# Four small edits to the order of a macaron encoder layer: one estimate for attention keys, a sum before splits, and the last two output units

## The chip, the cores and the metric

The kernel runs as one program on one core of a Trainium2 chip. The metric is the device time of one execution in microseconds (us). Engines are named as in the profile: PE is TensorE (PEld its weight loads), DVE is VectorE, ACT is ScalarE, POOL is GpSimd and SP is SyncE, which here only issues DMAs.

## The reference

One layer on 512 tokens of width 1024, all float32:

```python
h = modulate(rmsnorm(x, norm_ffn1), sh1, sc1)
x = x + 0.5 * g1 * swiglu(h, w_ffn1_in, w_ffn1_out)          # first block
h = modulate(rmsnorm(x, norm_mix), sh2, sc2)
qa, ka, va, qb, kb, vb, ga, gb = split(h @ w_in)
ya = window_gqa_sink(rope(rmsnorm(qa)), rope(rmsnorm(ka)), va, sink) @ w_branch_a
ob = diff_attention(rope(rmsnorm(qb)), rope(rmsnorm(kb)), vb, lam)
yb = (rmsnorm(ob) * (1 - lam_init)) @ w_branch_b
x = x + g2 * ((sigmoid(ga) * ya + sigmoid(gb) * yb) @ w_out)
h = modulate(rmsnorm(x, norm_ffn2), sh3, sc3)
x = x + 0.5 * g3 * swiglu(h, w_ffn2_in, w_ffn2_out)          # second block
```

The shifts, scales and gates `sh1` to `g3` come from `silu(c) @ w_mod + b_mod`; the inner width of both SwiGLU blocks is 2816.

## The kernel before

**Splits.** Each float32 operand of a matmul is split into a high part (ACT casts it) and a low part (DVE subtracts the cast from the source), and each product takes three matmuls: high by high, high by low, low by high. A weight chunk is loaded by SP into one of five `raw` buffers or into a `u4` buffer, cast (L481) and subtracted (L482) into one of five places of the pair `high`, `low`. A `u4` or `raw` chunk may then be changed in place by an accumulating DMA that POOL issues (L488), which makes the next weight sum out of it.

**Second block in units of seven products.** A `Unit` computes a 512 by 512 block of a product by Winograd's scheme: seven products (`s1`, `a11`, `a12`, `s2`, `s4`, `s3`, `a22`) in place of eight. `BANK` gives each product a PSUM bank: `a11`, `s2`, `s3` and `a22` of a unit are added up one after the other in bank `x`, `s1` and `s4` in `v`, `a12` in `w`. Between them bank `x` is read: ACT copies it after `a11` and `s2` (L510), and after `s3` DVE adds it to an earlier copy (L516), so that `a22` of the same unit can start only behind that sum. `after` holds these reads, `post` what becomes of a finished quarter. For the outgoing units `post` is in `out_unit` (L1706, one update of the residual stream per 128 rows, then a DMA to the output once a row block is complete).

**What sets the order there.** `items` is a list of products in the order in which PE does them. `run_items` walks it. `ASK` and `MAKE` say how many products ahead of its use a weight is loaded and split; `begin(starts[n])` issues what is due, and holds a split back while all five high/low places are taken. Only POOL's order is the program's; the order of PE, DVE, ACT and SP in the second block is made when the program is built, by a scheduler with estimates of its own. `copies` ties each weight cast behind the latest copy of a bank.

The list ends with the two outgoing units `end[0]` and `end[1]` (the last three row pairs of the hidden width, output rows 0 to 511 and 512 to 1023): both `s1` and both `a11` for the rows that are ready, the rest of these for the last row pair, then `a12`, `s2`, `s4`, `s3`, `a22`, each for both units in turn.

**Attention.** PE's, DVE's and ACT's order between the two blocks is written by `Line`, a list of pieces with due times in estimated us. Projections run as the main work, and a piece whose due time has come is put between two groups of their matmuls. `keys` normalises and rotates the keys of one block of 128 tokens and puts the turn of that block (a transpose on PE into the one bank `tp`, L1199, read by an ACT cast and a DVE subtract, L169 and L170) at `line.helped(...) + SLACK`, whose first number is the DVE time that is assumed. It serves the 8 key heads of the differential attention (`keys_b`, which runs first) and the 2 key heads of the window attention (`keys_a`, the second attention, under the projection `w_qa`).

Of the kernel before, what the change touches and what calls it, by code (L numbers as in the profile page):

```python
# [15 lines left out]
ALU = mybir.AluOpType  # L16
# [16 lines left out]
SH1, SC1, G1, SH2, SC2, G2, SH3, SC3, G3 = range(9)  # L33
# [64 lines left out]
RAW, HILO, F2 = 5, 5, 8  # L98
# [11 lines left out]
PERIOD_A, PERIOD_B, SLACK = 6.5, 3.6, 0.8  # L110
# [10 lines left out]
H = T // 2  # L121
# [3 lines left out]
def layer(ctx: ExitStack, tc: tile.TileContext, a: dict):  # L125
    nc = tc.nc
    V, S, G, PE = nc.vector, nc.scalar, nc.gpsimd, nc.tensor
# [14 lines left out]
    def f2():  # L142
        return sbuf("f2", [P, T], F32, F2)
# [10 lines left out]
    def bank(tag):  # L154
        return psum.tile([P, T], F32, name=name(tag), tag=tag, bufs={"acc": 3, "op": 1, "sc": 3, "tp": 1}[tag])
# [17 lines left out]
    turn, holders = [0], {}  # L173
# [11 lines left out]
    def let_go(holder):  # L185
        for i in [i for i in holders if holders[i] == holder]:
            del holders[i]
# [30 lines left out]
    begin = keep([P, 6 * NC], "begin")  # L218
    crow = u4(F32).rearrange("p a b -> p (a b)")[0:1, :]
    nc.scalar.dma_start(crow, a["c"].unsqueeze(0))  # L220
    x = [xt() for _ in range(NC)]
# [4 lines left out]
    parts, modv = [], []  # L226
# [198 lines left out]
    MAKE = {"s1": 5, "a11": 3, "a12": 2, "s2": 4, "s4": 2, "s3": 2, "a22": 3}  # L425
    T1, T2 = HALVES

    def two(po, w, k, x, first, last):

        (wh, wl), (xh, xl) = w, x  # L430
        for j in range(2):
            s = slice((2 * k + j) * P, (2 * k + j + 1) * P)
            out = po[:, j * H : (j + 1) * H]
            PE.matmul(out, wh[:, s], xh, start=first and j == 0, stop=False, skip_group_check=True)  # L434
            PE.matmul(out, wh[:, s], xl, start=False, stop=False, skip_group_check=True)  # L435
            PE.matmul(out, wl[:, s], xh, start=False, stop=last and j == 1, skip_group_check=True)  # L436

    copies = []

    class Unit:  # L440
# [8 lines left out]
            self.tags = {"w": "tp" if odd else "op"}  # L449

        asked = ("s1", "a11", "a12", "a22")
        copied = ()
        spare, apart, more = ("s1",), (), {"s1": ("s2", "a11"), "s2": ("s4", "a12"), "a11": ("s3", "a21")}

        def place(self, q):
# [35 lines left out]
        def multiply(self, q, ks=None):  # L491
            b = BANK[q]
            ks = range(self.depth) if ks is None else ks
            if b not in self.bank:
                self.bank[b] = bank(self.tags.get(b) or ("sc" if self.odd else "acc"))
            po = self.bank[b]
            new = not any(BANK[d] == b for d in self.done)
            for k in ks:
                x = self.operand(OPERAND[q], k)
                two(po, self.ready[q], k, x, new and k == 0, k == self.depth - 1)  # L500
            if self.depth - 1 in ks:
                let_go((self, q))

        def after(self, q):

            v, b = self.v, self.bank
            self.done.add(q)
            if q in ("a11", "s1", "s2"):
                v[q] = f2()
                copies.append(S.copy(v[q], b["v" if q == "s1" else "x"]).ins)  # L510
            elif q == "s3":
                t = b["x"]
                if q in self.copied:
                    t = f2()
                    S.copy(t, b["x"])
                V.tensor_tensor(v["s1"], v["s1"], t, ALU.add)  # L516
                self.post("c22", v["s1"], self)
            elif q == "a22":
                self.post("c21", b["x"], self)
            if q in ("a11", "a12") and self.done >= {"a11", "a12"}:  # L520
                V.tensor_tensor(v["a11"], v["a11"], b["w"], ALU.add)
                self.post("c11", v["a11"], self)
            if q in ("s2", "s4") and self.done >= {"s2", "s4"}:
                V.tensor_tensor(v["s2"], v["s2"], b["v"], ALU.add)
                self.post("c12", v["s2"], self)
# [3 lines left out]
    def run_items(items):  # L529

        at, due = 0.0, []
        starts = []
        for n, item in enumerate(items):
            starts.append(at)
            at += item[0]
            if item[1] is None:
                continue  # L540
            u, q = item[1:3]
            for do, ahead in ((u.ask, ASK), (u.prepare, MAKE)):
                if q in ahead:
                    due.append((starts[n] - PRODUCT * ahead[q] - 0.01, len(due), do, q))
        due.sort(key=lambda d: d[0:2])

        def begin(now):

            for d in [d for d in due if d[0] <= now]:
                _, _, do, p = d  # L550
                if do.__name__ == "ask" or p in do.__self__.ready or len(holders) < HILO:
                    due.remove(d)
                    do(p)

        for n, (cost, u, q, ks, also) in enumerate(items):
            begin(starts[n])
            if also is not None:
                also()
            if u is None:
                q()  # L560
                continue
            u.multiply(q, ks)
            begin(starts[n])
            if ks is None or u.depth - 1 in ks:
                u.after(q)


    SUMS = {"n1": ("b11", "b12"), "n2": ("n1", "b22"), "t4": ("n2", "b21"), "t3": ("b22", "b12")}
# [132 lines left out]
    ahead = []  # L701
# [542 lines left out]
    def keys(raw, nh, tabs, t, then):  # L1244
        rs = small(nh)
        z = head_stats(raw, nh, rs, False)
        y = rope(raw, nh, tabs, t, z)
        y3 = y[:, 0 : nh * HD].rearrange("p (h d) -> p h d", d=HD)
        if nh == 2:
            y, o = z, z[:, 0 : 2 * P].rearrange("p (h w d) -> p h w d", w=2, d=HD)  # L1250
            V.tensor_tensor(
                o, y3.unsqueeze(2).broadcast_to([P, nh, 2, HD]),
                rs.unsqueeze(2).unsqueeze(3).broadcast_to([P, nh, 2, HD]), ALU.mult,
            )
        else:
            y = wide_heads()
            V.tensor_tensor(y[:, :, 0, :], y3, rs.unsqueeze(2).broadcast_to([P, nh, HD]), ALU.mult)
        due = line.helped(0.4 * nh, 2.5) + SLACK
        line.at(due, lambda: then(y, slice(t * P, (t + 1) * P)), ("tp",))


# [436 lines left out]
    def out_unit(part, g, final):  # L1698
        seen = {}

        def post(c, v, u):
            n, t = int(c[1]) - 1, int(c[2]) - 1
            for j in range(2):
                m = 4 * g + 2 * n + j
                xr = x[m][:, HALVES[t]]
                V.scalar_tensor_tensor(xr, v[:, j * H : (j + 1) * H], modv[G3][:, m : m + 1], xr, ALU.mult, ALU.add)  # L1706
                seen[m] = seen.get(m, 0) + 1
                if final and seen[m] == 2:
                    nc.sync.dma_start(a["out"][m], x[m])

        r = slice(part.start * 2 * P, part.stop * 2 * P)
        srcs = {q: a["w2o"][g, i][:, r] for i, q in enumerate(("a11", "a12", "a21", "a22"))}
        return Unit(srcs, len(part), act_operand, post, g)
# [194 lines left out]

    end = [out_unit(PARTS[-1], g, True) for g in range(2)]
    for v in end:  # L1910
        v.copied = ("s3",)
    for v, p in seq:
        item(v, "s1", rest=p is None)
        item(u, "a22")
# [81 lines left out]
```

## Time and profile before

| | |
|---|---|
| time, median of 3 runs | 1053.09 us (1052.79, 1053.09, 1056.16) |
| the profiled execution's own time | 1054.45 us |
| its span, first to last instruction | 1052.7 us |
| PE busy | 1037.4 us, 99% |
| DVE, ACT, POOL busy | 792.9, 591.3, 151.7 us |
| granted PE clock, mean | 1.000 |
| PE waits for DVE, longest | 1.2 us (L434), 0.9 us (L1199) |
| DVE busy from 1037.3 to 1047.5 us | 10.10 us of 10.20 |

The page gives busy time and the costliest groups. The view of waits names what an engine waited for, the timeline gives the single instructions with their starts, and a row of it ends with the idle time ahead of the instruction and what ended it. Starts are in us from the span's first instruction. Matmuls overlap: one of 256 columns takes 0.28 us and the next starts 0.113 us later, so a lost time on PE is read from the starts.

### The profile page before, as it was taken

Reading aid. Unit: us, or ns where it says so; the run is one execution under the profiler, and the core shown is the slowest. Engines: PE = TensorE matmul, PEld = TensorE weight load, DVE = VectorE, ACT = ScalarE, POOL = GpSimd, SP = SyncE. Lnnn points to the kernel's source line nnn. Section 1 sums busy time; section 2 is a strip of 40 time slices with the busy share of each in tenths; the row PEclk is TensorE's granted clock in tenths of the full one; section 3 lists DMA queues with packets and bytes.
Section 4 is the critical chain, followed back from the end, with each engine's and each line's share of the span. In section 5 each row is a group of like instructions: output and inputs, shape, how many; then the busy total and the mean of one; then the engine's idle time right before and its main releaser. Section 6 shows DMA issues by size and latency. Waiting matters only on the chain.

```text
span 1052.7 us, 18398 instructions
## 1 busy us (share of the span) xinstructions
PE 1037.4 (99%) x7216; PEld 952.2 (90%) x7216; DVE 792.9 (75%) x1421; ACT 591.3 (56%) x976; POOL 151.7 (14%) x166
## 2 busy tenths in 40 slices
PE   8999999999999999999999999999999999999997
PEld 6799899989998988888888888989999999999997
DVE  7988767687967844677964778995888777877777
ACT  6565235424653443787755878435867545655553
POOL 1100001001001100441012401001111111111210
PEclk9999999999999999999999999999999999999999
DMA  9977886788666384785358875795578999999964
GB/s 353 364 211 231 255 247 145 203 290 199 176 200 210 131 268 142 159 195 114 89 172 203 217 181 149 280 323 132 111 177 197 236 250 198 206 236 210 210 137 125
DMA packets 64760, 214.07 MB, mean 203 GB/s; under 512 B 7713, under 2 KB 9889, under 8 KB 64674
## 3 DMA queue, kind: packets, MB, share of 16 engines
q1 hardware_dynamic: 43920, 143.63, 39.7%
q0 software_dynamic: 18304, 65.02, 33.9%
q10 hardware_dynamic: 2450, 4.25, 1.1%
q8 instruction: 56, 0.92, 0.4%
q14 instruction: 30, 0.25, 0.1%
HBM read 203.96 MB, written 8.92 MB: 202 GB/s over the span
## 4 chain that ended last, share of the span: by engine, by line
PE 88%; DVE 5%; ACT 3%; DMA 1%; issue 1%; POOL 1%; SPq 0%; DVEq 0%; ACTq 0%; POOLq 0%
PE acc L436 7%; PE acc L434 7%; PE acc L435 7%; PE sc L436 6%; PE sc L434 6%; PE sc L435 6%; PE sc L166 5%; PE sc L164 5%; PE sc L165 5%; PE acc L164 3%; PE acc L165 3%; PE acc L166 3%; PE acc L1148 2%; PE acc L1150 2%; PE acc L1149 2%; PE tp L1199 1%
## 5 line engine op out<-in xcount | busy, mean ns | idle before, releaser
L436 PE MATMUL acc<-b,low 128*128 128x256 f32 x614 | 170.1, 277 | 0.2 <-DVE low L170 0.2
L434 PE MATMUL acc<-b,high 128*128 128x256 f32 x614 | 170.0, 277 | 0.1
L435 PE MATMUL acc<-b,high 128*128 128x256 f32 x614 | 169.9, 277 | 0.2 <-DVE b L1776 0.2
L434 PE MATMUL sc<-b,high 128*128 128x256 f32 x542 | 149.9, 277 | 1.2 <-DVE f L516 1.2
L436 PE MATMUL sc<-b,low 128*128 128x256 f32 x542 | 150.0, 277 | 0.1
L435 PE MATMUL sc<-b,high 128*128 128x256 f32 x542 | 149.8, 276 | 0.0
L436 PEld LDWEIGHTS acc<-b,low 128*128 128x128 f32 x614 | 115.3, 188 | 0.7 <-DVE low L170 0.6
L435 PEld LDWEIGHTS acc<-b,high 128*128 128x128 f32 x614 | 115.3, 188 | 0.5 <-DVE b L1776 0.4
L434 PEld LDWEIGHTS acc<-b,high 128*128 128x128 f32 x614 | 115.4, 188 | 0.4 <-issue 0.3
L434 PEld LDWEIGHTS sc<-b,high 128*128 128x128 f32 x542 | 101.8, 188 | 1.4 <-issue 1.3
L436 PEld LDWEIGHTS sc<-b,low 128*128 128x128 f32 x542 | 101.7, 188 | 0.3 <-DVE low L801 0.3
L435 PEld LDWEIGHTS sc<-b,high 128*128 128x128 f32 x542 | 101.8, 188 | 0.0
L164 PE MATMUL sc<-b,high 128*128 128x512 f32 (+1 forms) x272 | 99.1, 364 | 0.0
L166 PE MATMUL sc<-b,low 128*128 128x512 f32 (+1 forms) x272 | 98.8, 363 | 0.2 <-DVE low L895 0.2
L165 PE MATMUL sc<-b,high 128*128 128x512 f32 (+1 forms) x272 | 98.9, 364 | 0.0
L482 DVE TENSOR_TENSOR low<-raw,high 128x1024 fp32r<-128x1024 f32 (+1 forms) x60 | 70.2, 1187 | 34.9 <-ACT high L481 34.8
L164 PE MATMUL acc<-b,high 128*128 128x512 f32 (+1 forms) x200 | 72.6, 363 | 0.2 <-DVE f L1597 0.2
L482 DVE TENSOR_TENSOR low<-u,high 128x1024 fp32r<-128x1024 f32 (+1 forms) x47 | 55.8, 1188 | 22.4 <-ACT high L481 22.2
L166 PE MATMUL acc<-b,low 128*128 128x512 f32 (+1 forms) x200 | 71.8, 359 | 0.0
L165 PE MATMUL acc<-b,high 128*128 128x512 f32 (+1 forms) x200 | 71.8, 359 | 0.0
L269 DVE CUSTOM_DVE_ANT_0 u<-u,ka,begin 128x1024 f32<-128x1024 f32 x45 | 58.6, 1310 | 12.4 <-DMA u<-w_mod 12.3
L481 ACT CAST high<-raw 128x1024 fp32r<-128x1024 f32 (+1 forms) x60 | 59.6, 1021 | 0.3 <-PE acc L435 0.3
(403 smaller groups left out, 2791.4 us busy)
## 6 DMA issues: line engine op xcount, KB each, us to landing
u<-w_mod SPq DMA_DIRECT2D x66, 512.0 KB, 6.0
raw<-w2i SPq DMA_DIRECT2D x31, 512.0 KB, 5.2
u<-w2i POOLq DMA_DIRECT2D x31, 512.0 KB, 7.4
raw<-w1u SPq DMA_DIRECT2D x27, 512.0 KB, 5.7
u<-w1u POOLq DMA_DIRECT2D x18, 512.0 KB, 7.7
raw<-w1o SPq DMA_DIRECT2D x16, 512.0 KB, 4.4
raw<-w_gate SPq DMA_DIRECT2D x16, 512.0 KB, 4.1
low<-w_gate POOLq DMA_DIRECT2D x13, 512.0 KB, 7.3
```

Of the source, the lines that this page charges most:

```text
L164: PE.matmul(out, wh, xh, start=first, stop=False)
L165: PE.matmul(out, wh, xl, start=False, stop=False)
L166: PE.matmul(out, wl, xh, start=False, stop=last)
L269: summed = V.tensor_tensor_reduce(out=w, in0=w, in1=cact, scale=by, scalar=b, op0=ALU.mult, op1=ALU.add, accum_out=t,)
L434: PE.matmul(out, wh[:, s], xh, start=first and j == 0, stop=False, skip_group_check=True)
L435: PE.matmul(out, wh[:, s], xl, start=False, stop=False, skip_group_check=True)
L436: PE.matmul(out, wl[:, s], xh, start=False, stop=last and j == 1, skip_group_check=True)
L481: S.copy(hi, t)
L482: V.tensor_tensor(lo, t, f(hi), ALU.subtract)
L1148: PE.matmul(out[t][:, 0:n], hh[k][:, ht], wh[:, o : o + n], start=k == 0, stop=False)
L1149: PE.matmul(out[t][:, 0:n], hh[k][:, ht], wl[:, o : o + n], start=False, stop=False)
L1150: PE.matmul(out[t][:, 0:n], hl[k][:, ht], wh[:, o : o + n], start=False, stop=k == NC - 1)
```

## The change

Four edits:

1. In `keys`, the assumed DVE time goes from `0.4 * nh` to `1.3 + 0.25 * nh`: for 8 heads from 3.2 to 3.3, for 2 heads from 0.8 to 1.8.
2. In `run_items`, behind product `s3` the sum on its bank (`after`) is issued ahead of the loads and splits that are due (`begin`), where it was issued behind them.
3. For the two last outgoing units `a12` is put among the `apart` weights: its high and low parts go into a `b8` buffer of its own and not into one of the five places. It is asked for 8 products ahead in place of 5 and split 5 ahead in place of 2. `begin` lets such a split pass when the five places are taken.
4. `end[1]` is `halved`: its bank `x` becomes two banks of 256 columns. Each product into it runs all of its matmuls for the first 128 output rows, then all for the second; every copy of the bank becomes two (`copy_out`); and after `a22` each half has its own update, issued as soon as its own matmuls are.

```diff
-    def two(po, w, k, x, first, last):
+    def two(po, w, k, x, first, last, js=range(2)):
         (wh, wl), (xh, xl) = w, x
-        for j in range(2):
+        for j in js:
             s = slice((2 * k + j) * P, (2 * k + j + 1) * P)
-            out = po[:, j * H : (j + 1) * H]
-            PE.matmul(out, wh[:, s], xh, start=first and j == 0, stop=False, skip_group_check=True)
+            out = po[j] if isinstance(po, list) else po[:, j * H : (j + 1) * H]
+            PE.matmul(out, wh[:, s], xh, start=first and j == js[0], stop=False, skip_group_check=True)
...
     def multiply(self, q, ks=None):
+            halves = self.halved and b == "x"
             if b not in self.bank:
-                self.bank[b] = bank(self.tags.get(b) or ("sc" if self.odd else "acc"))
+                tag = self.tags.get(b) or ("sc" if self.odd else "acc")
+                self.bank[b] = [bank(tag)[:, 0:H] for j in range(2)] if halves else bank(tag)
...
-            for k in ks:
-                x = self.operand(OPERAND[q], k)
-                two(po, self.ready[q], k, x, new and k == 0, k == self.depth - 1)
+            for js in ((0,), (1,)) if halves else (range(2),):
+                for k in ks:
+                    x = self.operand(OPERAND[q], k)
+                    two(po, self.ready[q], k, x, new and k == 0, k == self.depth - 1, js)
+                if halves and q == "a22":
+                    self.post("c21", po[js[0]], self, js)
...
+        def copy_out(self, b):
+            t, po = f2(), self.bank[b]
+            if self.halved and b == "x":
+                for j in range(2):
+                    done = S.copy(t[:, j * H : (j + 1) * H], po[j])
+            else:
+                done = S.copy(t, po)
+            return t, done.ins
...
-            for do, ahead in ((u.ask, ASK), (u.prepare, MAKE)):
+            for do, ahead in ((u.ask, {**ASK, **u.asks}), (u.prepare, {**MAKE, **u.makes})):
...
-                if do.__name__ == "ask" or p in do.__self__.ready or len(holders) < HILO:
+                u = do.__self__
+                if do.__name__ == "ask" or p in u.ready or p in u.apart or len(holders) < HILO:
...
             u.multiply(q, ks)
-            begin(starts[n])
+            if q != "s3":
+                begin(starts[n])
             if ks is None or u.depth - 1 in ks:
                 u.after(q)
+            if q == "s3":
+                begin(starts[n])
...
-        due = line.helped(0.4 * nh, 2.5) + SLACK
+        due = line.helped(1.3 + 0.25 * nh, 2.5) + SLACK
...
     for v in end:
-        v.copied = ("s3",)
+        v.copied, v.apart = ("s3",), ("a12",)
+        v.asks, v.makes = {"a12": 8}, {"a12": 5}
+    end[1].halved = True
```

What this does to the order in which the engines' instructions stand is shown at three places. Line numbers of the changed program are 1 higher in `prepare` and 15 to 20 higher further down.

**PE, the turns of the second attention's keys** (`tp` the bank, `ident` the identity, `f_613` and `f_616` the keys of the first two token blocks; `acc` and `sc` are the banks of the projection that runs meanwhile). Before:

```order
L1150 MATMUL sc_5460<-high,b_269_3292 128x512
L1199 MATMUL tp_5489<-ident,f_613_5394 128x128 x2
L1148 MATMUL sc_5460<-high,b_267_3290 128x512
...
L1150 MATMUL acc_5457<-high,b_269_3292 128x512
L1199 MATMUL tp_5510<-ident,f_616_5410 128x128 x2
L1148 MATMUL acc_5458<-high,b_267_3290 128x512
```

Changed:

```order
L1169 MATMUL sc_5460<-high,b_269_3292 128x512
L1218 MATMUL tp_5492<-ident,f_613_5394 128x128 x2
L1167 MATMUL acc_5457<-high,b_267_3290 128x512
...
L1169 MATMUL sc_5460<-high,b_269_3292 128x512
L1218 MATMUL tp_5525<-ident,f_616_5410 128x128 x2
L1167 MATMUL sc_5460<-high,b_267_3290 128x512
```

The first turn stands 3 matmuls later, and between the first and the second turn stand 21 matmuls where 9 stood. Between the second, third and fourth there are 9 each time, as before.

**DVE, the first `s3` of the second block** (`f_953` the copy that the sum is added to, `sc_7286` bank `x` of that unit, `u_942` a weight chunk). Before:

```order
L521 TENSOR_TENSOR f_959_7740<-f_959_7740,op_7779 128x512
L170 TENSOR_TENSOR b_966_7816<-f_964_7813,b_966_7816 128x256
L170 TENSOR_TENSOR b_967_7847<-b_926_7220,b_967_7847 128x2x256
L482 TENSOR_TENSOR low<-u_942_7490,high 128x1024
...
L516 TENSOR_TENSOR f_953_7650<-f_953_7650,sc_7286 128x512
```

Changed:

```order
L536 TENSOR_TENSOR f_959_7740<-f_959_7740,op_7779 128x512
L170 TENSOR_TENSOR b_966_7816<-f_964_7813,b_966_7816 128x256
L170 TENSOR_TENSOR b_967_7847<-b_926_7220,b_967_7847 128x2x256
L483 TENSOR_TENSOR low<-u_942_7490,high 128x1024
...
L531 TENSOR_TENSOR f_953_7650<-f_953_7650,sc_7286 128x512
```

Nothing moved: the split of `u_942` stands ahead of the sum in both. The row left out is a second half of `b_967`.

**ACT, the last two units** (`raw_10798` and `raw_10816` are the `a12` weights of `end[0]` and `end[1]` before, `raw_10737` and `raw_10767` in the change; `u_1114` and `u_1116` their `s2` weights; the copies read banks). Before:

```order
L510 COPY f_1140_10837<-sc_10770 128x512
L481 CAST high<-raw_10798 128x768
L481 CAST high<-u_1114_10419 128x768
L169 CAST b_1136_10800<-f_1132_10766 128x256
L510 COPY f_1141_10853<-acc_10785 128x512
L481 CAST high<-raw_10816 128x768
L481 CAST high<-u_1116_10486 128x768
```

Changed (the first two rows stand earlier):

```order
L482 CAST b_1137_10802<-raw_10737 128x768
L1674 ACTIVATE f_1128_10653<-f_1128_10653 128x512
...
L482 CAST b_1141_10822<-raw_10767 128x768
...
L517 COPY f_1143_10844<-sc_10774 128x512
L482 CAST high<-u_1114_10419 128x768
L169 CAST b_1138_10805<-f_1134_10770 128x256
L517 COPY f_1144_10858<-acc_10789 128x512
L482 CAST high<-u_1116_10486 128x768
L169 CAST ka_10864<-f_1134_10770 128x256
```

The two casts of `a12` left the place behind the copies and stand 9 and 6 rows further up; their subtractions on DVE moved with them. SP's and POOL's DMAs stand in the same order in both programs.

More of the change, by code (lines that the diff above doesn't have):

```diff
@@ L426, in layer @@
     T1, T2 = HALVES
-    def two(po, w, k, x, first, last):
+    def two(po, w, k, x, first, last, js=range(2)):
         (wh, wl), (xh, xl) = w, x
-        for j in range(2):
+        for j in js:
             s = slice((2 * k + j) * P, (2 * k + j + 1) * P)
-            out = po[:, j * H : (j + 1) * H]
-            PE.matmul(out, wh[:, s], xh, start=first and j == 0, stop=False, skip_group_check=True)
+            out = po[j] if isinstance(po, list) else po[:, j * H : (j + 1) * H]
+            PE.matmul(out, wh[:, s], xh, start=first and j == js[0], stop=False, skip_group_check=True)
             PE.matmul(out, wh[:, s], xl, start=False, stop=False, skip_group_check=True)
-            PE.matmul(out, wl[:, s], xh, start=False, stop=last and j == 1, skip_group_check=True)
+            PE.matmul(out, wl[:, s], xh, start=False, stop=last and j == js[-1], skip_group_check=True)
     copies = []
@@ L451, in layer @@
         asked = ("s1", "a11", "a12", "a22")
-        copied = ()
+        copied, halved = (), False
+        asks, makes = {}, {}
         spare, apart, more = ("s1",), (), {"s1": ("s2", "a11"), "s2": ("s4", "a12"), "a11": ("s3", "a21")}
@@ L508, in after @@
             if q in ("a11", "s1", "s2"):
-                v[q] = f2()
-                copies.append(S.copy(v[q], b["v" if q == "s1" else "x"]).ins)
+                v[q], done = self.copy_out("v" if q == "s1" else "x")
+                copies.append(done)
             elif q == "s3":
@@ L513, in after @@
                 if q in self.copied:
-                    t = f2()
-                    S.copy(t, b["x"])
+                    t, _ = self.copy_out("x")
                 V.tensor_tensor(v["s1"], v["s1"], t, ALU.add)
                 self.post("c22", v["s1"], self)
-            elif q == "a22":
+            elif q == "a22" and not self.halved:
                 self.post("c21", b["x"], self)
@@ L1699, in out_unit, with post @@
         seen = {}
-        def post(c, v, u):
+        def post(c, v, u, js=range(2)):
             n, t = int(c[1]) - 1, int(c[2]) - 1
-            for j in range(2):
+            for j in js:
                 m = 4 * g + 2 * n + j
                 xr = x[m][:, HALVES[t]]
-                V.scalar_tensor_tensor(xr, v[:, j * H : (j + 1) * H], modv[G3][:, m : m + 1], xr, ALU.mult, ALU.add)
+                y = v[:, j * H : (j + 1) * H] if len(js) > 1 else v
+                V.scalar_tensor_tensor(xr, y, modv[G3][:, m : m + 1], xr, ALU.mult, ALU.add)
                 seen[m] = seen.get(m, 0) + 1
```

## The prediction

> **What bounds the kernel now.** I read the page first, then PE's waits, then the timeline at the places that the four edits touch.
>
> ```profile
> PE 1037.4 (99%) x7216; PEld 952.2 (90%) x7216; DVE 792.9 (75%) x1421; ACT 591.3 (56%) x976; POOL 151.7 (14%) x166
> ```
>
> TensorE is busy 99% of the span, with a mean granted clock of 1.000: it sets the time. The change leaves its matmuls as they are in number and size (6938 rows of PE in both programs), so it can gain only where PE waits and behind PE's last matmul. The waits of PE, longest first (the last number is the longest single one):
>
> ```profile
> PE sc L590 <- DMA u<-c: 2.3, 1, 2.3
> PE acc L654 <- ACT b L336: 1.4, 2, 0.8
> PE sc L434 <- DVE f L516: 1.2, 1, 1.2
> PE tp L1199 <- DVE u L170: 0.9, 1, 0.9
> PE op L436 <- DVE low L482: 0.5, 1, 0.5
> ```
>
> The first two lie ahead of everything that is edited. The other three are each the place of one edit: `tp` is the bank of the keys' turns, L516 the sum behind `s3`, and `op` the bank of `a12` of `end[0]`. They are 2.6 us together; what stands behind PE's last matmul comes on top.
>
> **Edit 1, the keys' turns.** Second attention, 128-token blocks:
>
> ```profile
> 561.29 0.37 ACT L169 CAST ka<-tp 128x256 fp32r<-128x256 f32 x1 [0.80 <-PE tp L1199]
> 561.75 1.06 ACT L1085 ACTIVATE low<-raw 128x1024 fp32r<-128x1024 f32 x1
> 562.72 1.03 ACT L1084 CAST high<-raw 128x1024 fp32r<-128x1024 f32 x1
> 562.72 0.39 PE L1149 MATMUL acc<-low,b 128*128 128x512 f32 x1
> 562.94 0.40 PE L1150 MATMUL acc<-high,b 128*128 128x512 f32 x1
> 563.42 0.42 DVE L1251 TENSOR_TENSOR f<-f,sm 128x256 f32<-128x256 f32 x1 [0.25 <-POOL sm L1178]
> 563.76 0.42 DVE L170 TENSOR_TENSOR u<-tp,ka 128x256 fp32r<-128x256 f32 x1
> 564.23 0.44 PE L1199 MATMUL tp<-ident,f 128*128 128x128 f32 x2 [0.89 <-DVE u L170]
> ```
>
> The second turn needs the one bank `tp`, which DVE has read only at 564.2, behind the normalising of later blocks. PE's last matmul started at 562.94; at a pace of 0.227 (twice the 0.113 of 256 columns; the start before was 0.22 earlier) the turn could have started at 563.17, so 564.23 − 563.17 = **1.06 us** are lost. In the changed order the first turn comes 3 matmuls later (about 561.6), the second 21 matmuls after it in place of 9: 21 × 0.227 + 0.44 puts it at about 566.8. The first turn's cast then falls behind the 1.06 of L1085, ending near 563.1, and DVE's subtract behind 563.42 + 0.42 ends by about 564.3. That leaves 2 us of room, and the wait is gone. Late next are the third and fourth turns, which stay 9 matmuls (9 × 0.227 = 2.0 us) apart; the pair of ACT splits that is due there is this:
>
> ```profile
> 568.87 1.06 ACT L1085 ACTIVATE low<-raw 128x1024 fp32r<-128x1024 f32 x1 [1.48 <-PE sc L1149]
> ```
>
> It would stand ahead of the third turn's cast: 568.87 + 0.97 (to the next start, as from 561.75 to 562.72) + 0.37 + 0.42 gives 570.6, before the fourth turn at about 571.2. I take −1.06; bounds 0 (the wait comes back whole at a later turn) and −1.3 (a pace that is 0.005 slower for some dozens of matmuls behind the stall goes too).
>
> For the 8 heads the due time moves by 0.1 us, and a turn moves by one group at most. Its nearest wait is this one, a copy that must leave the bank before the turn writes it:
>
> ```profile
> 440.67 0.60 ACT L1215 COPY f<-acc 128x512 f32<-128x512 f32 x1
> 441.33 0.66 PE L1199 MATMUL acc<-ident,u 128*128 128x128 f32 x4
> ```
>
> The copy ended 0.06 ahead of the turn here; a turn one group (3 × 0.227 = 0.68) earlier would press on it, a later one would not. I take 0 of ±0.3.
>
> **Edit 2, the sum ahead of a split.** The first `s3` of the second block:
>
> ```profile
> 773.94 1.05 ACT L481 CAST high<-u 128x1024 fp32r<-128x1024 f32 x1 [2.45 <-DMA u<-w2i]
> 775.03 1.23 DVE L482 TENSOR_TENSOR low<-u,high 128x1024 fp32r<-128x1024 f32 x1 [1.90 <-ACT high L481]
> 776.15 0.28 PE L436 MATMUL acc<-b,low 128*128 128x256 f32 x1
> 776.77 0.68 DVE L516 TENSOR_TENSOR f<-f,sc 128x512 f32<-128x512 f32 x1
> 777.60 0.36 PE L434 MATMUL sc<-b,high 128*128 128x256 f32 x1 [1.17 <-DVE f L516]
> ```
>
> PE lost 777.60 − 776.15 − 0.113 = 1.34 us here because the sum of 0.68 us stands behind the split of 1.23, which waits for a cast that waits for a load. The edit says that the sum goes first. The order of the changed program says otherwise: on DVE the split of `u_942` still stands ahead of the sum, since not the place in the code but the scheduler's estimate of when each is ready decides. So 0; the bounds are 0 and −1.34.
>
> **Edits 3 and 4, the end.** ACT and DVE before `s2` of the last units:
>
> ```profile
> 1024.75 0.84 ACT L481 CAST high<-raw 128x768 fp32r<-128x768 f32 x1
> 1025.49 0.83 ACT L481 CAST high<-u 128x768 fp32r<-128x768 f32 x1
> 1025.62 0.96 DVE L482 TENSOR_TENSOR low<-raw,high 128x768 fp32r<-128x768 f32 x1 [2.63 <-ACT high L481]
> 1026.49 0.95 DVE L482 TENSOR_TENSOR low<-u,high 128x768 fp32r<-128x768 f32 x1
> 1026.63 0.38 PE L436 MATMUL op<-b,low 128*128 128x256 f32 x1 [0.49 <-DVE low L482]
> 1027.74 0.84 ACT L481 CAST high<-u 128x768 fp32r<-128x768 f32 x1
> 1027.74 0.87 POOL L488 DMA_DIRECT2D u<-w2o  x1 [10.28 <-DVE low L482]
> 1030.30 0.86 POOL L488 DMA_DIRECT2D u<-w2o  x1 [1.69 <-DVE ka L170]
> 1032.96 0.84 ACT L481 CAST high<-u 128x768 fp32r<-128x768 f32 x1 [3.60 <-DMA u<-w2o]
> 1035.22 0.84 ACT L481 CAST high<-u 128x768 fp32r<-128x768 f32 x1 [0.94 <-DMA u<-w2o]
> ```
>
> This is a chain. The split of `s2` (`u`, 1026.49) stands behind that of `a12` (`raw`). Only when DVE has read the `u` chunk does POOL issue the accumulating DMA that turns it into `s4`'s weight. It lands some 5 us later, and ACT, which works in order, casts it (1032.96 and 1035.22) and only then the four `raw` chunks of `s3` and `a22`. From 1037.3 on, DVE is the bound (columns: the stretch, its us, then busy us and instructions of PE, PEld, DVE, ACT, POOL, then clock, DMA share and GB/s):
>
> ```profile
> 1037.30:1047.50 10.20, 10.20 (x88) 10.08 (x87) 10.10 (x18) 3.35 (x5) 0.00 (x0) 1.00 0.27 104
> 1047.30 0.28 PE L436 MATMUL sc<-ka,low 128*128 128x256 f32 x1
> 1047.61 0.88 DVE L1706 SCALAR_TENSOR_TENSOR x<-sc,mod,x 128x256 f32<-128x256 f32 x2
> ```
>
> DVE is full for 18 instructions, 10.1 us, ends them at 1047.48, and the last two updates end at 1048.49; the rest of the span is the last DMA. So a gain counts only where both PE and this DVE queue end earlier.
>
> With `a12` split early, the first `s2` cast starts at 1024.75 in place of 1025.49 (−0.74), and the second loses both `a12` casts ahead of it (−1.46, to about 1026.28). The wait of PE in `op` goes, and with it the slow pace behind it:
>
> ```profile
> 1025.00:1034.80 9.80, 9.26 (x78) 8.84 (x77) 7.38 (x12) 5.69 (x10) 1.73 (x2) 1.00 0.69 122
> ```
>
> Of these 78 matmuls three began before 1025.00; 75 × 0.113 = 8.5, so PE lost 1.3 us here. POOL: the DMAs are issued at about 1026.9 and 1028.7 in place of 1027.74 and 1030.30. The cast of the first landed 1032.96 − 1027.74 = 5.2 after its issue, that of the second 4.9: 1032.1 and 1033.6. So the chain behind the second, and the DVE queue with it, starts 1.46 to 1.6 earlier and ends near 1046.0. Edit 4: the first half's 9 matmuls of `a22` are read while the other 9 run (9 × 0.113 = 1.02), so the update of the first half follows the queue at once. Behind the queue stand 0.40 (start to start) + 0.48 (the last): 1046.0 + 0.9 = 1046.9 in place of 1048.49, **−1.6**. PE's last matmul ends at 1047.30 − 1.3 + 0.31 = 1046.3, just ahead of the last update at 1046.4. The three copies more are ACT's, which is idle two thirds of this stretch.
>
> The bounds: if the second DMA lands as late as now, only the 0.1 of edit 4 is left: 1047.48 + 0.88 = 1048.36, −0.1. If DVE's queue gives way and PE decides, 1046.3 + 0.48 = 1046.8, −1.7.
>
> The Trainium skill ("PSUM — Partial Sum Buffer", section "Terms") says that two engines must not access one bank at once; by that alone two banks would free the first update 1.02 us ahead of PE's end. The row of DVE's full 10.10 us is against counting this whole.
>
> **Sum.** −1.06 + 0 + 0 − 1.6 = −2.66. The profiled execution took 1054.45 us (span 1052.7 and 1.75 around it), 1.36 above the median of 1053.09; the edits are the same for any execution, so I take 1053.09 − 2.66 = **1050.4 us**.
>
> **The rivals.** First, **the tail is hidden**: the accumulating DMA sets it. For it: these transfers take 4.9 and 5.2 us for 384 KB, and in the row of DMAs below POOL's kind is 1.7 us longer than SP's. An earlier one meets the load of `a22`'s weight, which the early `a12` split also lets go earlier. Against it: SP's load would then be issued well ahead, about 1015. It gives 1053.09 − 1.06 − 0.1 = 1051.9.
>
> ```profile
> u<-w2o POOLq DMA_DIRECT2D x6, 384.0 KB, 5.5
> raw<-w2o SPq DMA_DIRECT2D x6, 384.0 KB, 3.8
> ```
>
> The Trainium skill ("DMA: Bandwidth & Descriptors", section "Anatomy of one DMA — SWDGE (gpsimd) path") fits 2.0 us plus bytes over 436e3: an estimate of 2.9 us for 384 KB, by which nothing would wait for this DMA, PE would bound the end and the sum would be 1050.3. The 5.5 us measured is against it.
>
> Second, **the sum does move** (or the stall at 777 goes by a shift upstream): 1050.4 − 1.34 = 1049.1. Against it stands the unchanged order of DVE. Third, **the keys' wait moves on** to the third or fourth turn, whose distances are unchanged and whose ACT pair of 1.06 and 1.03 falls between them: 1.06 come back, 1050.4 + 1.06 = 1051.5. Fourth, on the other side, **the early `a12` blocks ACT**. Its cast now stands ahead of the SiLU of a hidden unit:
>
> ```profile
> 1001.25 0.33 SPq L463 DMA_DIRECT2D raw<-w2o  x1
> 1013.07 0.63 ACT L1655 ACTIVATE f<-f 128x512 f32<-128x512 f32 x1 [0.88 <-DVE f L524]
> ```
>
> ACT works in order: if the load is late, the SiLU and all that it feeds are late. The cast's place is at about 1012.2; the load is issued at 1001.25 and takes 3.8 us, so 7 us are to spare. Beyond 1012.2 each us costs one; from 2.7 us more the kernel is slower than before, and at 1018.5 (13.5 us behind the usual landing) it would be 1050.4 + 6.3 = 1056.7. Nothing in these rows is that late.
>
> **How the numbers follow.** Chances: my forecast 0.60, the tail hidden 0.15, the sum moved 0.10, the keys' wait moved on 0.10, ACT blocked 0.05. About 0.3%, 3.2 us, is what a measurement of this kernel can tell from no change, so faster means below 1049.9 and slower above 1056.3. The forecast's own bounds are 1049.9 (tail −1.7, keys −1.3, 8 heads −0.2) to 1051.2 (half of the tail's gain missing); a fifth of its 0.60 falls under 1049.9, 0.13, with the 0.10 for the sum moved and 0.03 out of the scatter of the executions: faster 0.26. Slower is most of the blocked ACT: 0.04. Same is the rest, 0.70. The range of 8 in 10 leaves the blocked ACT and the lower edge of the sum moved outside: 1049.0 to 1052.3.
>
> **What would show it.** Edit 1 is right if PE's wait at L1199 of the keys (0.9) is gone and no turn from 566 to 572 waits. Edit 2 is judged by the wait of `sc` on the sum: I expect it unchanged, 1.2. Edit 3 is right if the wait in `op` is gone and POOL's last two DMAs are issued 0.9 and 1.6 earlier against PE's progress. Edit 4 is right if the last updates are two of 128x256 close behind a DVE queue that ends about 1.5 earlier. The prediction is wrong if that queue starts no earlier, if PE waits for `s4`'s weights at about 1034 (their low part would be ready within 0.15 us of PE's wish), or if ACT's SiLU at 1013 waits.

## The result, and the profile after

| | before | changed |
|---|---|---|
| time, median (22 runs each) | 1054.44 us (1052.03 to 1058.33) | 1052.51 us (1049.78 to 1055.19) |
| ratio to before, 95% interval | | 0.9982 (0.9973 to 0.9990) |
| profiled execution: span | 1052.7 us | 1050.9 us |
| PE busy | 1037.4 us | 1035.8 us |

The change is 1.9 us faster (1.0 to 2.9), 0.18% of the time. The forecast was 2.7 us less and a time of 1050.4 in 1049.0 to 1052.3; the measured median lies 0.2 us above that range. The forecast gain lies inside the measured interval. The base that it was taken from was off: the three runs shown had a median of 1053.09, and 22 runs have one of 1054.44.

The page of the changed kernel, and then PE's waits there (total us, times, longest):

```profile
span 1050.9 us, 18397 instructions
PE 1035.8 (99%) x7216; PEld 951.5 (91%) x7216; DVE 792.6 (75%) x1421; ACT 591.7 (56%) x979; POOL 151.3 (14%) x166
```

```profile
PE sc L609 <- DMA u<-c: 2.9, 1, 2.9
PE acc L673 <- ACT b L336: 1.4, 2, 0.8
PE sc L434 <- DVE f L531: 1.3, 1, 1.3
...
PE acc L1167 <- ACT f L1116: 0.4, 1, 0.4
```

The waits at the second key turn (0.9) and in the bank of `a12` (0.5) are gone. The wait on the sum behind the first `s3` stands as it was, 1.3 in place of 1.2. A wait of 0.4 on L1116 is new and lies ahead of all that was edited: at 379 ACT came late out of the issue of its own DMAs (idle for 2.37 us ahead of its row at 379.37, for 1.88 before).

**Keys.** The timeline of the changed kernel at the turns, and then the same two PE instructions around that stretch, before and in the change:

```profile
561.91 0.38 PE L1218 MATMUL tp<-ident,f 128*128 128x128 f32 x2
562.84 0.36 ACT L169 CAST ka<-tp 128x256 fp32r<-128x256 f32 x1
563.82 0.42 DVE L170 TENSOR_TENSOR u<-tp,ka 128x256 fp32r<-128x256 f32 x1
566.94 0.38 PE L1218 MATMUL tp<-ident,f 128*128 128x128 f32 x2
569.24 0.38 PE L1218 MATMUL tp<-ident,f 128*128 128x128 f32 x2
571.53 0.38 PE L1218 MATMUL tp<-ident,f 128*128 128x128 f32 x2
```

```profile
544.26 0.36 PE L1150 MATMUL acc<-high,b 128*128 128x256 f32 x1
587.57 0.60 PE L1199 MATMUL acc<-ident,b 128*128 128x128 f32 x4
```

```profile
544.62 0.36 PE L1169 MATMUL acc<-high,b 128*128 128x256 f32 x1
586.79 0.60 PE L1218 MATMUL acc<-ident,b 128*128 128x128 f32 x4
```

DVE has read the bank at 564.2, as before; the second turn now comes at 566.94, and no later turn waits. The stretch went from 43.31 to 42.17 us: −1.14.

**The sum behind the first `s3`**, changed kernel:

```profile
773.03 1.05 ACT L482 CAST high<-u 128x1024 fp32r<-128x1024 f32 x1 [2.60 <-DMA u<-w2i]
774.11 1.23 DVE L483 TENSOR_TENSOR low<-u,high 128x1024 fp32r<-128x1024 f32 x1 [2.04 <-ACT high L482]
775.85 0.68 DVE L531 TENSOR_TENSOR f<-f,sc 128x512 f32<-128x512 f32 x1
776.68 0.36 PE L434 MATMUL sc<-b,high 128*128 128x256 f32 x1 [1.32 <-DVE f L531]
```

It is the same picture as before: load, cast, split, then the sum.

**The end**, changed kernel:

```profile
1022.48 0.59 ACT L517 COPY f<-acc 128x512 f32<-128x512 f32 x1 [1.73 <-PE acc L436]
1025.76 0.86 POOL L489 DMA_DIRECT2D u<-w2o  x1 [9.17 <-DVE low L483]
1027.59 0.86 POOL L489 DMA_DIRECT2D u<-w2o  x1 [0.97 <-DVE ka L170]
1030.62 0.84 ACT L482 CAST high<-u 128x768 fp32r<-128x768 f32 x1 [3.76 <-DMA u<-w2o]
1033.34 0.83 ACT L482 CAST high<-u 128x768 fp32r<-128x768 f32 x1 [1.40 <-DMA u<-w2o]
1035.49 1.83 DVE L483 TENSOR_TENSOR low<-raw,high 128x768 fp32r<-128x768 f32 x2 [0.33 <-ACT high L482]
1045.34 0.28 PE L436 MATMUL sc<-ka,low 128*128 128x256 f32 x1
1045.57 0.87 DVE L1726 SCALAR_TENSOR_TENSOR x<-sc,mod,x 128x256 f32<-128x256 f32 x2
```

Counted from ACT's copy behind `s1` of `end[0]` (1022.48; 1023.59 before), POOL's two accumulating DMAs are issued 3.28 and 5.11 us later, where it was 4.15 and 6.71. So the second comes 1.6 us earlier, as worked out. But its cast comes at 10.86 in place of 11.63, only 0.8 earlier: the transfer took 5.75 us from issue to cast in place of 4.92. The last update ends at 1046.44, which is 23.96 behind the copy, where it was 24.90: −0.94.

By the starts of equal instructions, the 1.8 us of the two spans came about so: +0.36 up to 544 (mostly the late ACT at 379), −1.14 at the keys, −0.28 in small waits from 587 to the sum, +0.14 at the sum, −0.19 between the sum and the copy, −0.94 from the copy to the last update, +0.25 behind it.

### The profile page after: what moved, and what is told of

It is laid out like the page before. It is cut to its first block, busy times and chain, and to the rows that moved or that the text cites. A ratio compares the mean times of both kernels' runs of the same rounds, so it can differ in the third digit from the quotient of the medians.

```text
span 1050.9 us, 18397 instructions
## 1 busy us (share of the span) xinstructions
PE 1035.8 (99%) x7216; PEld 951.5 (91%) x7216; DVE 792.6 (75%) x1421; ACT 591.7 (56%) x979; POOL 151.3 (14%) x166
## 4 chain that ended last, share of the span: by engine, by line
PE 74%; issue 9%; DVE 7%; DMA 4%; ACT 3%; POOL 2%; ACTq 0%; SPq 0%; POOLq 0%; DVEq 0%
PE sc L166 5%; PE sc L164 5%; PE sc L165 5%; PE sc L434 5%; PE sc L436 5%; PE sc L435 5%; PE acc L434 4%; PE acc L436 4%; PE acc L435 4%; PE acc L164 3%; PE acc L165 3%; PE acc L166 3%; PE acc L1167 2%; PE acc L1169 2%; PE acc L1168 2%
## 5 line engine op out<-in xcount | busy, mean ns | idle before, releaser
L482 ACT CAST high<-u 128x1024 fp32r<-128x1024 f32 (+1 forms) x47 | 48.0, 1023 | 20.1 <-DMA u<-w2o 5.6
```

Source lines behind the costliest of these rows:

```text
L482: S.copy(hi, t)
```

## The experiments

Three questions: is each edit's share what its place in the trace says; why did the second transfer take longer; and what makes the base move by more than the edits gain? The theory on record at the start: edit 1 removes the second turn's wait, edit 2 does nothing, edits 3 and 4 shorten the end until late `s4` weights or PE bound it.

### Edit 1 for the two key heads alone

```diff
-        due = line.helped(0.4 * nh, 2.5) + SLACK
+        due = line.helped(1.8 if nh == 2 else 0.4 * nh, 2.5) + SLACK
```

> The kernel before with edit 1 for the two key heads of the window attention alone (0.8 to 1.8); the 8 heads keep 3.2. Theory (the whole of edit 1 is the wait at the second turn): PE's wait of 0.9 us at the keys' turn is gone, no new one stands between 560 and 590, and the stretch from the last matmul start near 544 to the turn near 587 is 43.3 - 1.1 = 42.2 us, as it is with all edits; time -1.0 to -1.2 us against the kernel before, less than the measurement can tell. Rival (the wait moves to the third or fourth turn): the stretch stays at 43.3.

Measured: 0.9991 of the kernel before (0.9980 to 1.0003), −1.0 us; its interval includes no change, as foreseen. The wait of 0.9 at the turn does not stand in its list of waits, and the stretch from the matmul near 544 to the turn near 587 is 42.18 us: the theory's 42.2, as in the change. So the gain of edit 1 there is this wait. For the 8 heads, the stretch from 428.62 to 465.11 (before) went to 36.36 from 36.49 us in the change, −0.1.

The wait is not the same in every execution. In the six profiles without edit 1 it is 0.27 to 0.89 us and the stretch 42.69 to 43.31; in the eight with it, the stretch is 42.17 to 42.38. On the mean edit 1 is worth 0.75 us. The profile that the forecast was made from has the longest wait of the six.

### Edits 3 and 4 alone

The diff is the change without its parts in `keys` and `run_items` (the `begin` behind `s3`).

> The kernel before with edits 3 and 4 alone. Measure: from ACT's copy behind s1 of end[0] (1023.59 before) to the end of the last update is 24.90 us before and 23.96 with all edits. Theory (the end does not depend on edits 1 and 2): 23.9 to 24.1 here, and the keys' wait of 0.9 and the wait of 1.2 to 1.3 on the sum behind s3 stay; time -0.7 to -1.0 us. Rival (the four edits act on each other, by shifting the end against the loads): more than 0.3 us away from 23.96.

Measured: 0.9987 (0.9971 to 1.0003), an interval that includes no change. From the copy to the last update 23.61 us, 0.35 below the 23.96 of the change, so by its own words the rival holds, by a hair. The likelier reading is scatter: the second transfer took 5.41 us here and 5.75 in the change, which is the same difference, 0.34. The keys' wait (0.6) and that on the sum (1.0) stand. The gain at the end is there without edits 1 and 2.

### The sum really held ahead

```diff
             if copies:
                 with tc.issue_after(copies[-1]):
                     S.copy(hi, t)
-                V.tensor_tensor(lo, t, f(hi), ALU.subtract)
+                if sums:                        # the sum behind the first s3
+                    with tc.issue_after(sums[-1]):
+                        V.tensor_tensor(lo, t, f(hi), ALU.subtract)
+                else:
+                    V.tensor_tensor(lo, t, f(hi), ALU.subtract)
...
```

`sums` holds the sum behind the first `s3` for the splits that are issued behind it, up to and with those due at the start of the next product.

> The changed kernel with one more tie: the split of the u weight that stands ahead of the sum behind the first s3 is held behind that sum on DVE, which edit 2 was to do and did not. Theory (the sum waits only for the split of 1.23 us, which waits for its load): PE's wait of 1.2 to 1.3 on the sum is gone, 1.3 to 1.5 us less between 770 and 790, and nothing later is late, since the split is used five products on; time -1.3 us against the changed kernel. Rival (the sum is late for its own bank or for the casts ahead of it, or the later split delays its user): the wait stays above 0.5 or a wait of about the same size turns up behind it.

Measured: 0.9965 of the kernel before (0.9953 to 0.9978). Against the change, each by the ratio to its own base, that is 1.8 us better (1.4 by the medians); the two intervals overlap a little. PE lost nothing between 770 and 795. DVE and ACT of this kernel:

```profile
770.53 1.05 ACT L482 CAST high<-u 128x1024 fp32r<-128x1024 f32 x1 [1.02 <-DMA u<-w2i]
772.34 0.68 DVE L535 TENSOR_TENSOR f<-f,sc 128x512 f32<-128x512 f32 x1
772.94 1.22 DVE L485 TENSOR_TENSOR low<-u,high 128x1024 fp32r<-128x1024 f32 x1
```

The sum now stands ahead of the split. Edit 2 changes no order here: the traces with edits 3 and 4 alone and with all four have the same order of instructions on DVE, ACT, POOL and SP in the second block. The split in question was issued behind the sum in the kernel before as well: a tie that takes hold only of splits issued behind the sum takes hold of it there too (the run with the tie alone, below). The scheduler had put it ahead. A place in the code does not bind it; a tie does. But this weight landed early here, so the execution alone does not show the wait removed.

### The whole end earlier, with the sum held

```diff
-        v.asks, v.makes = {"a12": 8}, {"a12": 5}
+        v.asks, v.makes = {"a12": 8}, {"a12": 5, "s2": 5, "s3": 5}
```

> The changed kernel with the sum held ahead as in the run before, and for the last two units s2 split 5 products ahead (4 before) and s3 split 5 ahead (2 before), into the places that a12 no longer takes. Theory (the end is bound by the late s4 weights and by DVE's queue behind them): the accumulating DMAs start 0.6 and 1.5 us earlier, two splits of 0.87 us leave DVE's queue, PE bounds the end, and from ACT's copy to the end of the last update it is 23.2 to 23.6 us in place of 23.96; with the sum -1.7 to -2.1 us against the changed kernel, -3.5 to -4.0 against the one before (0.35%). Rival (PE already bounds the end): 23.9, and only the 1.3 of the sum.

Measured: 0.9960 (0.9945 to 0.9975), at the median 0.7 us below the run before. Its end:

```profile
1042.48 0.88 DVE L1733 SCALAR_TENSOR_TENSOR x<-acc,mod,x 128x256 f32<-128x256 f32 x2
1043.50 0.48 DVE L1733 SCALAR_TENSOR_TENSOR x<-sc,mod,x 128x256 f32<-128x256 f32 x1
1044.20 0.28 PE L436 MATMUL sc<-ka,low 128*128 128x256 f32 x1
1044.52 0.48 DVE L1733 SCALAR_TENSOR_TENSOR x<-sc,mod,x 128x256 f32<-128x256 f32 x1 [0.54 <-PE sc L436]
```

DVE now waits for PE: the first half is updated 1 us ahead, and the second right behind PE's last matmul. So PE bounds the end, as the theory said, but the end came no earlier for it: from the copy to the last update it is 23.64 us, just outside the 23.2 to 23.6 expected, and the run before, with the old splits, has 23.43. Against the copy, the second accumulating DMA was issued 1.0 us earlier than in the change, not 1.5. What is gained lies behind the last update: 3.6 us in place of 4.4, the size of the 0.7 at the median. The likely reason, not tested by itself, is that the last two row blocks no longer leave together.

### The second transfer by itself

```diff
-                G.dma_start(t, self.srcs[src], accum_op=ALU.add)
+                if not (self.skip and q == "s2"):      # skip: end[0] only
+                    G.dma_start(t, self.srcs[src], accum_op=ALU.add)
```

> The changed kernel without the accumulating DMA that makes the s4 weight of end[0] (that product then takes the s2 weight, so the output rows of end[0] are another thing); the one of end[1] is left alone in POOL's queue. With both, the second one takes 5.2 to 5.75 us from its issue to the cast when it is issued 1.8 us behind the first, and 4.9 when 2.6 behind it. Theory (the two transfers share the 16 DMA engines, so that the second lands some 2.3 to 2.7 us behind the first, whenever it was issued): alone it takes 4.3 to 4.9. Rival (the 5.2 to 5.75 is its own time, whatever runs beside it): 5.2 or more again.

POOL's issue and ACT's cast of the transfer left:

```profile
1027.82 0.86 POOL L490 DMA_DIRECT2D u<-w2o  x1 [10.71 <-DVE low L483]
1032.59 0.84 ACT L482 CAST high<-u 128x768 fp32r<-128x768 f32 x1 [0.47 <-DMA u<-w2o]
```

4.77 us: the theory's range, not the rival's. In the changed kernel, with both under way, the stretch from 1028 to 1031 of its DMA view reads:

```profile
DMA packets 173, 0.48 MB, mean 161 GB/s; under 512 B 16, under 2 KB 16, under 8 KB 173
q0 software_dynamic: 173, 0.48, 97.7%
```

POOL's queue holds 97.7% of the 16 engines there and moves 161 GB/s, at which 384 KB take an estimated 2.4 us. So the second of two such transfers lands some 2.4 us behind the first, whether it is issued 1.5 or 2.6 us behind it: in the eight profiles with edit 3 and both transfers the two casts lie 2.2 to 3.0 us apart, in the five without edit 3 2.3 to 2.5. Issuing it earlier moved it no further than the first one allowed.

### Edits 3 and 4 taken apart

Edit 3 alone (the change's `apart`, `asks` and `makes`, no `halved`):

> The kernel before with edit 3 alone. From ACT's copy behind s1 of end[0] to the end of the last update it is 24.7 to 24.9 us before and 23.4 to 24.0 in three runs with edits 3 and 4. Theory (edit 3 carries the gain, by the earlier s2 splits; edit 4 gives 0.1 while DVE's queue is the bound and 0.4 once PE is): 23.8 to 24.1. Rival (edit 4 carries half of it or more): 24.3 or more.

It came to 24.29, between the two and at the rival's edge. Here the second transfer took 6.1 us and PE waited for its low part:

```profile
1028.47 0.86 POOL L489 DMA_DIRECT2D u<-w2o  x1 [0.96 <-DVE ka L170]
1034.61 0.83 ACT L482 CAST high<-u 128x768 fp32r<-128x768 f32 x1 [1.71 <-DMA u<-w2o]
1036.49 0.39 PE L436 MATMUL sc<-b,low 128*128 128x256 f32 x1 [0.22 <-DVE low L483]
1046.78 0.87 DVE L1723 SCALAR_TENSOR_TENSOR x<-sc,mod,x 128x256 f32<-128x256 f32 x2
```

Edit 4 alone (`end[1].halved = True` and what it needs):

> The kernel before with edit 4 alone. Same measure. Theory (DVE's queue of 10.1 us stands ahead of both updates): 24.6 to 24.8, 0.1 less than before, and PE's wait of 0.5 in the bank of a12 stays. Rival (the first half is read 1 us ahead of PE's end): 24.0 or less.

It came to 24.74, inside the theory's range; four profiles without edits 3 and 4 have 24.90, 24.83, 24.73 and 24.72, so the 0.1 of edit 4 cannot be told from nothing. DVE works through to the last update without a pause:

```profile
1044.53 0.87 DVE L1723 SCALAR_TENSOR_TENSOR x<-acc,mod,x 128x256 f32<-128x256 f32 x2
1045.32 0.87 DVE L1723 SCALAR_TENSOR_TENSOR x<-sc,mod,x 128x256 f32<-128x256 f32 x2
```

So against a mean of 24.8 they gave 0.5 and at most 0.1 alone, and together 0.8 to 1.4. What makes the difference is when the second transfer lands (us; the cast is ACT's of that transfer, the end is that of the last update):

| | second transfer, issue to cast | copy to cast | cast to end |
|---|---|---|---|
| before; before, again | 4.9; 4.8 | 11.63; 11.55 | 13.27; 13.28 |
| keys alone; tie alone | 5.0; 5.0 | 11.69; 11.66 | 13.04; 13.06 |
| edit 4 alone | 4.9 | 11.64 | 13.10 |
| edit 3 alone | 6.1 | 11.25 | 13.04 |
| changed | 5.8 | 10.86 | 13.10 |
| edits 3 and 4 | 5.4 | 10.51 | 13.10 |
| sum held ahead | 5.2 | 10.33 | 13.10 |
| the end earlier | 5.8 | 9.87 | 13.77 |
| one transfer left out | 4.8 | 9.58 | 13.82 |

From that cast to the end it takes 13.0 to 13.3 us, with edit 4 or without, as long as the cast comes 10.3 us or more behind the copy; where it comes earlier, DVE waits for PE and the end follows PE. So edit 3 brings the gain, as far as the landing lets it, and the lesser gain of edit 3 alone is the late landing of that execution. A gain of edit 4 is not seen in any of these; what it is worth where PE is the bound was not run without it.

### The kernel before once more, and its scatter

> The kernel before once more, to see what one execution differs by from the next. Theory (the forecast's base was a lucky median: executions scatter by where transfers land): the span is within 2 us of 1052.7, and the stages that differ are those that wait for a load: the first load of c (2.3 to 3.0 us in five profiles), the u weight ahead of the sum behind s3 (PE lost 0.4 to 1.5 us), ACT's own DMA issue near 379. The keys' wait of 0.9 at the second turn should stand again, within 0.4, and the end should take 24.7 to 24.9. Rival (the scatter lies in PE's pace or in the clock): the same waits as before, and the difference spread over the whole span.

The span was 1053.3. The end (24.83) stands as before, and the keys' wait again, at 0.7. What differs most is what waits for loads: `c` 2.9 in place of 2.3 (of which 0.4 is still there at 31 us), PE's loss at the sum 1.25 in place of 1.63, and a second wait on such a sum at 884 (0.5).

These two executions differ by 0.6 us only, and none above 1055.1 us was profiled, so the slowest are not explained by a trace. There is one sign that the rival may have a part in them: in the three later series of the kernel before, 9 of the 11 executions above 1056 us list a mean granted clock of 0.998 or less, and 2 of the 44 below. In every profile here the clock is below full only behind PE's last matmul (in the change 0.50 from 1048 on, with the last matmul at 1045.34); whether it falls earlier in the slow executions, or is the mark of a long wait in them, is open.

The load ahead of the first sum is an accumulating DMA of 512 KB. Here is its time from POOL's issue to ACT's cast, in all profiles, and PE's loss between 770 and 795 against an even pace:

| without the tie | us | PE loss | with the tie | us | PE loss |
|---|---|---|---|---|---|
| edit 4 alone | 5.8 | 0.0 | tie for all sums | 6.0 | 0.0 |
| one transfer left out | 6.2 | 0.0 | sum held ahead | 6.6 | 0.0 |
| keys alone | 6.6 | 0.5 | all together | 7.7 | 0.0 |
| edits 3 and 4 | 7.8 | 1.2 | output in halves | 8.0 | 0.0 |
| before, again | 7.8 | 1.3 | the end earlier | 9.0 | 0.0 |
| before | 8.0 | 1.6 | tie alone | 10.3 | 1.4 |
| changed | 8.1 | 1.6 | | | |
| edit 3 alone | 8.3 | 1.7 | | | |

In these eight profiles without the tie PE loses some 0.7 us for each us of this load beyond 6; with it nothing up to 9. The issue and the cast of the first and the last row:

```profile
765.46 0.86 POOL L489 DMA_DIRECT2D u<-w2i  x1 [6.57 <-DVE low L483]
771.23 1.05 ACT L482 CAST high<-u 128x1024 fp32r<-128x1024 f32 x1 [0.23 <-DMA u<-w2i]
```

```profile
765.12 0.86 POOL L492 DMA_DIRECT2D u<-w2i  x1 [6.56 <-DVE low L486]
775.44 1.05 ACT L481 CAST high<-u 128x1024 fp32r<-128x1024 f32 x1 [4.78 <-DMA u<-w2i]
781.53 0.38 PE L436 MATMUL acc<-b,low 128*128 128x256 f32 x1 [0.28 <-DVE low L486]
787.49 0.35 PE L434 MATMUL acc<-b,high 128*128 128x256 f32 x1 [0.46 <-DVE f L520]
```

The last of these comes from the next run, the kernel before with the tie and none of the edits:

> The kernel before with the one tie alone: on DVE the split that stands ahead of the sum behind the first s3 is held behind it; none of the four edits. Ten profiles so far: PE lost 0 to 1.7 us at this sum without the tie (nothing when the u weight landed early) and nothing in both runs with it, and the times of those two spread over 2.1 and 2.5 us where those of the kernel before spread over 6.1. Theory (where this weight lands makes a good part of the scatter of the kernel before): the wait is gone, the median is 1 to 2.5 us below the kernel before, and the spread of a dozen times falls below 4 us. Rival (the scatter is from elsewhere, and the tie wins its 1.2 us only): median -1.2, spread 5 us or more as before.

Measured: 0.9990 (0.9981 to 0.9998), −1.1 us; twelve times from 1051.33 to 1054.03, a spread of 2.7, beside 6.6 for the kernel before on the same chip (1051.51 to 1058.11, 19 runs). The median moved by no more than the rival said, the spread fell as the theory said. Its profile, of the slowest of the twelve, shows what is left: at 10.3 us of load the sum is in time, but what ACT and DVE do behind that cast is late. PE waits at 781.5 for the low part of a later split and at 787.5 for the sum behind the next unit's `s3`, and loses 1.4 in all.

### More of the same

The tie for every `s3` of the second block but the last two, on top of the end made earlier:

```diff
-                if self is lead:
+                if self not in end:
                     sums.append(done.ins)
```

> The best so far (sum held ahead, s2 and s3 of the last units split earlier) with the tie for every s3 of the second block except those of the last two units. In three of six profiles without it PE lost 0.4 to 0.6 us near 883 at another such sum. Theory: that loss goes too where it stood, 0 to -0.6 us against the best so far (0.9960 of the kernel before), 0.9955 to 0.9960. Rival: the splits held back are late for their own products, and a new wait of over 0.5 us on a low part stands in the second block; 0.9965 or more.

Measured: 0.9962 (0.9946 to 0.9977), no difference from 0.9960, no new wait; seven times within 0.6 us. The loss near 883 that it was to take away had been in three of ten profiles, not of six as the expectation says, so it had little to win.

The output rows of the last units in halves, on top of the end made earlier:

```diff
-                if final and seen[m] == 2:
-                    nc.sync.dma_start(a["out"][m], x[m])
+                if final:
+                    nc.sync.dma_start(a["out"][m][:, HALVES[t]], xr)
```

> The best so far, and the output rows of the last units leave in halves of 128 KB as soon as each is updated, 16 DMAs in place of 8. From the end of the last update to the end of the span it is 3.6 us in the best and 4.2 to 4.5 in the kernels before and changed; about 1.05 MB leave there in 2.7 us, of which half is final 4 us earlier. Theory (what is left behind the last update is the queue of output): -0.3 to -0.7 us, 0.9953 to 0.9957 of the kernel before. Rival (it is the latency of the last DMA alone, or SP's issue of twice as many): no change or up to +0.5 us.

Measured: 0.9959 (0.9944 to 0.9974), a median of 1049.41. From the last update to the end of the span 3.2 us in place of 3.6: the lower edge of the theory, and too small to be told from nothing by the times alone.

All of it together:

> Everything that helped together: the four edits, the split held behind every such sum, s2 and s3 of the last units split earlier, output in halves. The two steps added last were worth next to nothing (0.9962 against 0.9960) and little (0.9959) by themselves, with intervals of 0.0015 to each side. Theory (the sums held ahead take out waits that depend on a landing, so the times lie close together): 0.9950 to 0.9960 of the kernel before, and a spread of 1.5 us or less over its times. Rival (the held splits cost what they save): 0.9962 or more, spread over 2 us.

Measured: 0.9952 (0.9935 to 0.9969), a median of 1049.28 in 1049.03 to 1050.26: 5 us below the kernel before in that run, with an interval that lies wholly below 1 and below that of the change (0.9973 to 0.9990).

## Why the prediction was right or wrong

- **The base, wrong.** The step that failed is the last of the sum: the profiled 1054.45 was "1.36 above the median of 1053.09; the edits are the same for any execution, so I take 1053.09". The three runs shown spread over 3.4 us, and 22 over 6.3 with a median of 1054.44; that this is also the profiled execution's own time is chance. With that base the same sum gives 1051.8, inside the range. The range has no term for the base; of the scatter only 0.03 went into the chance of faster. The median of three was a low draw, and the four times at hand, with the profiled one, have a mean of 1054.1. What makes the times scatter is known in part: the forecast priced the stall at the sum as a constant 1.34 us, and PE's loss there is 0 to 1.7.
- **The prices, from one execution.** Of the forecast 2.66 us, 1.9 were measured. On the mean of the profiles edit 1 is worth 0.75, and edits 3 and 4 shorten the end by 1.1 (24.8 to 23.7) and lengthen what stands behind it by 0.1: 1.8 in all.
- **Edit 1, the mechanism right.** −1.06 was taken, and −1.14 measured between the two profiles shown; the second turn was placed at 566.8, and stands at 566.94 on a clock that is 0.36 late; the 8 heads were put at 0 ± 0.3, and are −0.1. No wait moved on to the third or fourth turn. But the wait of 0.9 was the longest of six, so that −1.06 is more than the mean.
- **Edit 2, right.** Nothing moved, as the order said. The rival price of −1.34 was of the right kind: the tie that does hold the sum ahead brought 1.4 to 1.8 us on top of the change and 0.8 to 1.1 alone.
- **Edits 3 and 4, the mechanism right, a term mis-sized.** −1.6 was taken; −0.94 was measured in that profile, and −0.8 to −1.4 in three with both edits against the mean of 24.8 before. Issue times came out as worked out (0.9 and 1.6 earlier against the copy). The term that failed is "that of the second 4.9: 1032.1 and 1033.6": the second transfer was given the duration that it had when it was issued 2.56 us behind the first. Issued 1.83 behind, it took 5.2 to 6.1, and 4.77 alone. The two share the 16 engines, and the end follows its landing (the table above). This is the first rival's mechanism at a part of its price. PE, too, won 0.85 us from the copy to its last matmul, where the forecast let all of the 1.3 go. The Trainium skill's estimate ("DMA: Bandwidth & Descriptors", section "Anatomy of one DMA — SWDGE (gpsimd) path") of 2.9 us for 384 KB does not hold here for these accumulating transfers, even for one alone: 4.77 from issue to cast.
- **Edit 4, no gain seen.** It was priced at 0.1 while DVE's queue is full, and that cannot be told from nothing here. The 1.02 us between the two halves is seen only where PE became the bound (the updates at 1043.50 and 1044.52).
- **The blocked ACT did not come.** Between 995 and 1024 us, where it would show, PE waits for nothing in any profile.
- The likeliest class was no change clear of the measurement (0.70), and it came out so, at −0.18%.

## What to carry to other kernels

A median of three runs is not a base when their spread is larger than the forecast gain: take the spread into the range, and ask which wait makes it. A wait read from one execution may be its longest. When a transfer is issued earlier, it lands earlier only as far as the transfer ahead of it on the same engines allows: size the pair, not the one. And a statement's place in the code does not order an engine whose order a scheduler makes; tie the instruction, and look at the order that comes out.

## What the runs showed that was not expected

The accumulating DMA of 512 KB took 5.8 to 10.3 us from issue to cast at the same place in fourteen profiles of nearly the same program; the median of such loads of that matrix is 7.4 in the kernel before, where SP's plain loads of the same size have 5.2. In the profiles without the tie PE lost 0 to 1.7 us behind it. Holding one subtract of 1.23 us behind one sum of 0.68 us goes with a narrower spread of the times: 2.7 us or less in all six kernels that had it (0.6 to 2.7), where those without it spread over 3.8 to 6.9 (6 to 12 times with it, 11 to 25 without). Five of the six have the other edits too; with the tie alone it was 2.7 against 6.6. The narrowing is measured, but its cause is not shown: a loss of up to 1.7 us does not make a spread of 6, and the wait of 0.3 to 0.5 at another sum near 884, in four of the twelve profiles without a tie there, says that this load is not the only source.
